# A hybrid decoder layer on one core: norm factors sent through DRAM, gate products in three split passes, and more of the down projection done in seven products of eight

## The chip, the cores and the metric

The kernel runs on one core of a Trainium2 chip. The metric is the device time of one launch in microseconds (us). Before the change it is 2038.34 us, the median of 3 runs (2037.39 to 2038.42). The profiled execution of the same kernel took 2035.2 us, of which 2033.4 us lie between its first and its last instruction (the span).

## The reference

One layer of a decoder is computed for 2048 prompt tokens and 8 single-token samples, 2056 rows of width 1024, all in float32:

```
xn = rmsnorm(x); z = xn @ w_in            # 1024 -> 1792: recurrent branch, gate branch, q, k, v
xc = causal_conv4(xr)
r, i = sigmoid(block_diag(xc, Wa)+ba), sigmoid(block_diag(xc, Wx)+bx)   # 8 blocks of 64 x 64
h_t = a_t h_(t-1) + sqrt(1-a_t^2) (i xc)_t ;  rec = h * gelu(gate)
att = sliding-window attention (self + 128 previous tokens, a sink per head)
mix = [rmsnorm(rec), rmsnorm(att)];  h = x + mix @ w_out
ff = silu(hn @ w_gate) * (hn @ w_up), hn = rmsnorm(h);  y = h + ff @ w_down     # 1024 -> 2816 -> 1024
out = rmsnorm(y)
```

An rmsnorm needs one factor for each token: the inverse root of the mean square of its 1024 (or 512) values.

## The kernel before

**Layout.** Channels lie on the 128 partitions and tokens along the free dimension. A norm factor belongs to a token, so it has to stand in every partition as a row. `rstd_cols` (L1013) sums the squares with TensorE into a column of factors (tokens on partitions); `row_bcast` (L1020) turns such columns into a row on all 128 partitions with one float32 matmul for each 128 tokens (the column spread over 128 weight columns, times the identity) and a ScalarE copy. `half_bcast` (L1042) does the same for the token halves of the feed-forward part.

**Products in split precision.** A float32 operand is split into a high part of type float32r and the rest, also float32r; a product is three matmuls that add up in PSUM: high times high, high times low, low times high. In the trace every matmul of float32r is one record, and a matmul of full float32 is two. The gates of the recurrence (`rec_chunk`, tiles `g`) were not split: one full float32 matmul for each of 40 pieces, 16 of 260 columns and 24 of 512.

**Part one** goes over four runs of tokens (520, 512, 512, 512): input projection (`ip`), convolution, gates, scan, attention (`s`, `pt`, `o`), the two group norms (`rc`, `at`), output projection (`op`), and the sum `h`, which goes to DRAM (`hs`).

**Part two** goes over three groups of tokens (688, 684, 684), each of two halves of 344 or 342 tokens, and in each group over 11 pairs of 128-row pieces of the feed-forward width. Gate and up products (`ps_g`, `ps_u`) take seven products where a two-by-two block product takes eight (the Strassen-Winograd form): 7 x 12 matmuls each, 168 for a pair. The seven sums of `hn` halves (`n`, stored as `mixed` in DRAM by `hn_mix`, read back by `hn_load`) and the seven sums of weight quarters are their operands. The down projection of a pair has two forms:

- `down` (tiles `pd`): the plain eight products, 16 outputs of 6 matmuls, 96 matmuls, and 16 VectorE additions into the running sum `y`. Its weights are split on ScalarE and on GpSimd (`w_d`).
- `down_parts` (tiles `pw`): seven products, 14 rounds of 6 matmuls, 84 matmuls, and 28 VectorE additions into `y`. It needs three more parts of `ff` made of sums (tiles `t`, by additions `c_u<-c_u,c_u`), and sums of weight quarters (`sd`, `rd`), which `down_make` adds up and stores (`sums_d`) and `down_load` reads back.

`wino(gi, p)` (L75) says which pair of which group takes the second form. Before: pairs 1 to 9 of groups 1 and 2; group 0 makes no such sums, group 1 makes and stores them, group 2 reads them. The rounds of pair p stand among the products of pair p+1, from product number `R_AT` on. The lists `E_...` say for each kind of addition whether VectorE (V) or GpSimd (P) does it.

**What sets the order.** All five queues (TensorE, VectorE, ScalarE, GpSimd, and SP, which issues nearly every DMA) run in an order that is written out in the table `ORDER`, one string for each engine; `w_x:17` means 17 instructions recorded under the name `w_x`, and `+2` takes the third one that is still open. Each engine takes its instructions strictly in this order; an instruction that waits holds all that stand behind it.

Of the kernel before, what the change touches and what calls it, by code (L numbers as in the profile page):

```python
# [7 lines left out]
F32 = mybir.dt.float32  # L8
F32R = mybir.dt.float32r
# [44 lines left out]
U_R, R_AT = 0.875, 2  # L54
# [13 lines left out]
E_DSUM = ['P', 'P', 'P', 'P', 'P', 'P', 'P', 'V']  # L68
# [6 lines left out]
def wino(gi, p):  # L75
    return gi > 0 and 0 < p < NPAIR - 1


def plan():
    t, begin, end, prod, down, rounds = T_B0, [], [], {}, {}, {}  # L80
    for gi in range(len(HALVES)):
        begin.append(t)
        for p in range(NPAIR):
            mixed = p and wino(gi, p - 1)
            n = 0
            for i in range(14):
# [12 lines left out]
        end.append(t)  # L99
# [18 lines left out]
vt0_2 ip0_13_0:13 ip0_13_1:6 vt0_3 ip0_13_1:16 ip0_2_0 ip0_13_1 ip0_2_0 ip0_13_1 ip0_2_0:4 s0_0_0:2 ip0_2_0:2 s0_0_0
ip0_2_0 s0_0_0 s0_0_1 ip0_2_0:3 s0_0_1:2 ip0_2_0:3 g0_0_0_0 ip0_2_0:4 s0_0_1 ip0_2_0:4 ip0_2_1:4 s0_1_0 ip0_2_0
ip0_2_1 s0_1_1 s0_1_0:3 ip0_2_1:2 s0_1_1:3 ip0_2_1:2 g0_0_0_260 ip0_2_1:10 s1_0_0 ip0_2_1 s1_0_0:2 ip0_2_1:2 s1_0_0  # L120
ip0_2_1 pt0_0_1 ip0_2_1 pt0_0_1:3 ip0_5_0:2 s1_0_1:2 ip0_5_0:2 s1_0_1:2 ip0_5_0:4 g0_0_1_0 ip0_5_0:10 o0_0_0 ip0_5_0:6
s1_1_0 ip0_5_1:2 s1_1_0:3 ip0_5_1:6 g0_0_1_260 ip0_5_1:3 pt0_1_1:3 ip0_5_1:3 pt0_1_1 o0_0_0 ip0_5_1:2 s1_1_1 ip0_5_1:4
s1_1_1 ip0_5_1 s1_1_1:2 ip0_5_1 ip0_4_0 ip0_5_1:2 ip0_4_0:3 s2_0_0:2 ip0_4_0 s2_0_0 ip0_4_0 s2_0_0 ip0_4_0:4 o0_1_0
ip0_4_0:6 o0_1_0 pt1_0_0 ip0_4_0 pt1_0_0 ip0_4_0:2 pt1_0_0 ip0_4_0:2 pt1_0_0 s2_0_1:4 ip0_4_0 ip0_4_1:2 ip0_4_0
ip0_4_1:6 ip0_4_0 ip0_4_1:16 ip1_8_0:12 ip0_6_0 ip1_8_0:3 ip0_6_0:5 o1_0_0 ip0_6_0:4 pt1_0_1:2 ip0_6_0 ip1_8_0 pt1_0_1
ip0_6_0 o1_0_0 pt1_0_1 g0_3_0_0 ip0_6_0:12 ip0_6_1 ip1_8_0 ip0_6_1:8 ip1_8_0 ip0_6_1:3 s2_1_0 ip0_6_1:3 s2_1_0 ip1_8_0
ip0_6_1 s2_1_0:2 ip0_6_1:4 s2_1_1 ip0_6_1:3 s2_1_1:2 o1_0_1 ip0_6_1 s2_1_1 g0_3_0_260 ip1_8_0:2 pt1_1_0 ip1_8_0
pt1_1_0:2 ip1_8_0 pt1_1_0 ip1_8_0 ip1_9_0:2 o1_0_1 ip1_9_0:9 g0_3_1_0 ip1_9_0:7 ip0_7_0:2 ip1_9_0 ip0_7_0:3 ip1_9_0
ip0_7_0:4 ip1_9_0:3 pt1_1_1:2 o1_1_0 ip1_9_0 ip0_7_0 pt1_1_1:2 o1_1_0 ip0_7_0:4 g0_3_1_260 ip0_7_0:7 s3_0_0 ip0_7_0:3
bc_x1_0 s3_0_0 o1_1_1 s3_0_1 s3_0_0 s3_0_1 s3_0_0 s3_0_1:2 bc_x1_0 pt2_0_0:2 bc_x1_0 pt2_0_0 o1_1_1 ip0_7_1 bc_x1_0  # L130
ip0_7_1:5 pt2_0_0 ip0_7_1:18 o2_0_0 ip1_10_0:4 g0_2_0_0 ip1_10_0:2 o2_0_0 pt2_0_1:3 ip1_10_0:7 pt2_0_1 ip1_10_0:11
ip1_11_0 o2_0_1 ip1_11_0:2 s3_1_0:4 pt2_1_0:2 g0_2_0_260 pt2_1_0 s3_1_1:3 pt2_1_0 ip1_11_0:2 s3_1_1 ip1_11_0 o2_0_1
ip1_11_0:11 pt2_1_1:2 g0_2_1_0 pt2_1_1 ip1_11_0:7 ip1_4_0:4 pt2_1_1 ip1_4_0:2 o2_1_0:2 g0_2_1_260 ip1_4_0:18 ip1_0_0
o2_1_1 ip1_0_0:2 vt1_0 ip1_0_0:5 pt3_0_0:2 ip1_0_0 dS:2 pt3_0_0:2 o2_1_1 ip1_0_0:3 dS ip1_0_0:2 dS:5 ip1_0_0:9 o3_0_0
ip1_12_0 ip1_0_0 dS2 ip1_12_0 dS2 ip1_12_0 pt3_0_1 ip1_12_0 pt3_0_1:2 o3_0_0 pt3_0_1 ip1_12_0:20 ip1_13_0:6 o3_0_1
ip1_13_0:2 o3_0_1 ip1_13_0:2 pt3_1_0:2 ip1_13_0 pt3_1_0 ip1_13_0 pt3_1_0 ip1_13_0:7 dS3 ip1_13_0:3 dS3 ip1_1_0
ip1_13_0:2 ip1_1_0:6 pt3_1_1 ip1_1_0 pt3_1_1:2 o3_1_0 ip1_1_0 pt3_1_1 ip1_1_0 dS4 o3_1_0 dS4 ip1_1_0 dS4 s4_0_0 dS4
ip1_1_0 o3_1_1 s4_0_1:3 s4_0_0:3 s4_0_1 dS4:4 o3_1_1 ip1_1_0:11 ip1_5_0:2 ip1_1_0 dS5 ip1_5_0:2 s4_1_0 dS5 s4_1_1
ip1_5_0 s4_1_1 ip1_5_0 s4_1_0 s4_1_1 ip1_5_0 s4_1_1 ip1_5_0 vt1_1 s4_1_0 ip1_5_0:2 s4_1_0 ip1_5_0:6 pt4_0_0:3
ip1_5_0:2 ip1_2_0 pt4_0_0 s5_0_0 ip1_2_0 s5_0_0:2 s5_0_1:3 s5_0_0 ip1_2_0:2 s5_0_1 vt1_2 ip1_2_0:8 pt4_0_1:4 o4_0_0  # L140
vt1_3 ip1_2_0:5 o4_0_0 ip1_2_0:2 pt4_1_0 st_rc0 ip1_2_0:2 pt4_1_0:3 st_rc0:4 s5_1_0 ip1_2_0:2 s5_1_0:3 ip1_2_0
# [2118 lines left out]
```

## Time and profile before

| what | us |
|---|---|
| median of 3 runs | 2038.34 |
| the profiled execution | 2035.2 |
| its span | 2033.4 |
| TensorE busy in it | 2004.7 |
| VectorE busy | 1472.9 |
| ScalarE busy | 955.0 |
| GpSimd busy | 906.8 |
| part one, until the last output products | 0 to about 663 |
| group 0 of part two, from there | to about 1135 |

Busy time is the union of an engine's instructions. TensorE's matmuls overlap each other (one of 344 columns is recorded with 320 ns, and the next starts 157 ns later), so what a matmul costs is read from the distance of starts or ends, or from the count of matmuls in a stretch, and not from its recorded duration. The granted clock of TensorE is 0.995 over the span.

### The profile page before, as it was taken

Reading aid. Unit: us, or ns where it says so; the run is one execution under the profiler, and the core shown is the slowest. Engines: PE = TensorE matmul, PEld = TensorE weight load, DVE = VectorE, ACT = ScalarE, POOL = GpSimd, SP = SyncE. Lnnn points to the kernel's source line nnn. Section 1 sums busy time; section 2 is a strip of 40 time slices with the busy share of each in tenths; the row PEclk is TensorE's granted clock in tenths of the full one; section 3 lists DMA queues with packets and bytes.
Section 4 is the critical chain, followed back from the end, with each engine's and each line's share of the span. In section 5 each row is a group of like instructions: output and inputs, shape, how many; then the busy total and the mean of one; then the engine's idle time right before and its main releaser. Section 6 shows DMA issues by size and latency. Waiting matters only on the chain.

```text
span 2033.4 us, 34750 instructions
## 1 busy us (share of the span) xinstructions
PE 2004.7 (99%) x12273; PEld 1904.5 (94%) x12273; DVE 1472.9 (72%) x2694; ACT 955.0 (47%) x1960; POOL 906.8 (45%) x799
## 2 busy tenths in 40 slices
PE   9999999999999999999999999999999999999997
PEld 8988887888778999999999999999999999999997
DVE  6888986777886777765555777787767666776675
ACT  5776764654563543443344533343335433433443
POOL 4312451120132796676666645565557422322333
PEclk9999999999999999999999999999999999999999
DMA  9863675667688776764546687776668675555552
GB/s 338 297 215 127 225 273 182 210 197 223 206 288 272 285 245 208 240 212 168 184 172 224 229 282 242 261 240 214 228 209 290 204 236 196 182 197 199 195 173 101
DMA packets 208991, 450.98 MB, mean 222 GB/s; under 512 B 25232, under 2 KB 82720, under 8 KB 208800
## 3 DMA queue, kind: packets, MB, share of 16 engines
q1 hardware_dynamic: 205184, 445.73, 65.2%
q10 hardware_dynamic: 3632, 3.02, 0.5%
q8 instruction: 97, 1.59, 0.3%
q14 instruction: 78, 0.64, 0.1%
HBM read 335.89 MB, written 113.84 MB: 221 GB/s over the span
## 4 chain that ended last, share of the span: by engine, by line
PE 88%; DMA 6%; DVE 4%; issue 1%; ACT 1%; SPq 0%; DVEq 0%; ACTq 0%
PE ps_g L963 20%; PE ps_u L963 20%; PE ip L963 14%; PE pw L963 12%; PE pd L963 11%; PE op L963 5%; PE s L963 1%; DMA m<-mixed 1%; PE g L963 1%; PE pt L968 1%; PE o L963 1%; DMA mixed<-n 1%; DMA y<-hs 1%; DMA xs<-in_xT 0%; DMA hn<-mixed 0%
## 5 line engine op out<-in xcount | busy, mean ns | idle before, releaser
L963 PE MATMUL ps_g<-hn,w_g 128*128 128x342 f32 (+1 forms) x2772 | 546.0, 320 | 1.8 <-DMA w_g<-split_g 1.0
L963 PE MATMUL ps_u<-hn,w_u 128*128 128x342 f32 (+1 forms) x2772 | 529.8, 320 | 4.5 <-ACT c_u L1985 3.5
L963 PEld LDWEIGHTS ps_u<-hn,w_u 128*128 128x128 f32 x2772 | 455.0, 189 | 5.5 <-ACT c_u L1985 3.8
L963 PEld LDWEIGHTS ps_g<-hn,w_g 128*128 128x128 f32 x2772 | 456.6, 189 | 2.5 <-ACT w_d L1778 2.3
L963 PE MATMUL ip<-xn,w_in 128*128 128x512 f32 (+1 forms) x1680 | 367.3, 361 | 3.9 <-ACT w_in L936 2.7
L963 PEld LDWEIGHTS ip<-xn,w_in 128*128 128x128 f32 x1680 | 271.5, 190 | 49.4 <-issue 4.8
L2050 DVE TENSOR_TENSOR y<-y,pw 128x342 f32<-128x342 f32 x504 | 242.7, 506 | 94.8 <-PE pw L963 90.4
L963 PE MATMUL pd<-fh,w_d 128*128 128x344 f32 (+1 forms) x960 | 235.0, 320 | 0.0
L963 PE MATMUL op<-mix,w_out 128*128 128x512 f32 (+1 forms) x960 | 209.8, 362 | 0.3 <-DVE mix L999 0.3
L2021 DVE TENSOR_TENSOR y<-y,pd 128x344 f32<-128x344 f32 (+1 forms) x240 | 119.6, 509 | 103.3 <-PE pd L963 91.1
L963 PEld LDWEIGHTS op<-mix,w_out 128*128 128x128 f32 x960 | 157.6, 190 | 30.0 <-issue 6.1
L963 PE MATMUL pw<-fh,wd 128*128 128x342 f32 x576 | 167.5, 319 | 1.0 <-DVE y L2021 1.0
L963 PEld LDWEIGHTS pd<-fh,w_d 128*128 128x128 f32 x960 | 167.3, 188 | 0.0
L963 PE MATMUL pw<-t,wd 128*128 128x342 f32 x648 | 150.6, 319 | 0.0
L963 PE MATMUL pd<-fl,w_d 128*128 128x344 f32 (+1 forms) x480 | 147.6, 320 | 0.0
L1946 POOL TENSOR_TENSOR c_u<-c_u,c_g 128x342 f32<-128x342 f32 (+1 forms) x60 | 58.8, 980 | 180.2 <-DVE c_u L1964 144.5
L1964 DVE TENSOR_TENSOR c_u<-c_u,ps_u 128x342 f32<-128x342 f32 (+1 forms) x99 | 50.5, 510 | 122.1 <-PE ps_u L963 121.8
L1935 DVE TENSOR_TENSOR fl<-c_u,fh 128x342 fp32r<-128x342 f32 (+1 forms) x132 | 118.5, 909 | 15.3 <-ACT fh L1934 14.2
L1779 POOL TENSOR_TENSOR w_u<-ru,w_u 128x512 fp32r<-128x512 f32 x44 | 58.9, 1340 | 151.8 <-ACT w_u L1778 123.0
L1934 ACT CAST fh<-c_u 128x342 fp32r<-128x342 f32 (+1 forms) x132 | 62.1, 479 | 106.4 <-POOL c_u L1946 41.9
L963 PEld LDWEIGHTS pw<-t,wd 128*128 128x128 f32 x648 | 111.4, 189 | 0.0
L963 PEld LDWEIGHTS pw<-fh,wd 128*128 128x128 f32 x576 | 105.6, 189 | 1.3 <-DVE y L2021 1.3
(299 smaller groups left out, 3499.9 us busy)
## 6 DMA issues: line engine op xcount, KB each, us to landing
w_g<-split_g SPq DMA_DIRECT2D x88, 512.0 KB, 4.4
w_u<-split_u SPq DMA_DIRECT2D x88, 512.0 KB, 5.5
w_in<-split_w SPq DMA_DIRECT2D x84, 512.0 KB, 3.6
rg<-in_wgate SPq DMA_DIRECT2D x110, 256.0 KB, 3.1
ru<-in_wup SPq DMA_DIRECT2D x110, 256.0 KB, 3.3
w_out<-split_w SPq DMA_DIRECT2D x48, 512.0 KB, 4.8
split_g<-w_g SPq DMA_DIRECT2D x44, 512.0 KB, 2.8
split_u<-w_u SPq DMA_DIRECT2D x44, 512.0 KB, 2.9
```

Of the source, the lines that this page charges most:

```text
L963: r = nc.tensor.matmul(*args, **kw)
L968: r = nc.tensor.transpose(*args)
L1779: lo_eng.tensor_tensor(w[:, 1, :], src, w[:, 0, :].bitcast(F32), op=ALU.subtract)
L1934: nc.scalar.copy(hi, v)
L1935: nc.vector.tensor_tensor(lo, v, hi.bitcast(F32), ALU.subtract)
L1946: (nc.vector if p == NPAIR - 1 or src is not v else eng(E_MUL[2 * h + n])).tensor_tensor(v, src, g, op=ALU.mult)
L1964: nc.vector.tensor_tensor(o, a, b, op)
L2021: nc.vector.tensor_tensor(ys[gi, n, m], ys[gi, n, m], ps, ALU.add)
L2050: nc.vector.tensor_tensor(v, v, ps, ALU.add)
```

## The change

**Norm factors.** A new helper, `rows_out`, turns the column of factors into rows with a single TensorE transpose, copies them on ScalarE and writes them to DRAM; `dram_bcast` reads such a row back with a DMA that repeats it on 128 partitions. It takes the place of `row_bcast` for the factors of `x` in token runs 1 to 3, of `rc` in runs 1 and 2, and of the finishing norm of groups 0 and 1. The factors of `h` are written to one row in DRAM (`rows_h`), from which `half_bcast` reads. 56 float32 matmuls go, 13 transposes come, with 13 small writes and 15 reads on SP's queue.

**Gates.** The gate weights are split once (`gwh`, `gwl`), each chunk `xc` is split by ScalarE and GpSimd (`xch`, `xcl`), and a gate piece is three float32r matmuls.

**Down projection.** `wino` now also holds for pair 0 of groups 1 and 2 and for pairs 3 to 9 of group 0. Group 0 makes and stores the weight sums of pairs 3 to 9; group 1 reads these and makes those of pairs 0 to 2; group 2 reads all. In group 0 the sums and splits alternate between VectorE and GpSimd. The rounds of pair 0 start at product number 6 of pair 1 (`R_FIRST`). In all, 864 matmuls `pd` become 756 `pw`.

The scratch that the compiler sets aside for dynamic DMAs is made smaller (2048), and the table `ORDER` is written anew for all engines.

```diff
-U_R, R_AT = 0.875, 2
+U_R, R_AT, R_FIRST = 0.875, 2, 6
...
-E_DSUM = ['P', 'P', 'P', 'P', 'P', 'P', 'P', 'V']
+E_DSUM = [['P', 'V', 'P', 'V', 'P', 'V', 'P', 'V'], ['P', 'P', 'P', 'P', 'P', 'P', 'P', 'V']]
+E_T0 = ['P', 'V', 'P', 'V']
+E_DLO0 = ['P', 'V', 'P', 'V', 'P', 'V', 'P']
...
 def wino(gi, p):
-    return gi > 0 and 0 < p < NPAIR - 1
+    return p < NPAIR - 1 and (gi > 0 or p >= 3)
...
-                if mixed and i >= R_AT:
+                if mixed and i >= (R_AT if p > 1 else R_FIRST):
...
+        rowp = E(tc.tile_pool(name="rowp", bufs=2))
...
+        rows_h = dp.tile([1, NTOK], F32, name="rows_h")
+
+        def rows_out(row, cols, w, nt, name):
+            ps = m_tile(f"tr_{name}")
+            tr(f"tr_{name}", ps[:nt, :w], cols, ident[:w, :w])
+            v = rowp.tile([8, P], F32, tag="row", name=f"row_{name}")[:nt, :w]
+            nc.scalar.copy(v, ps[:nt, :w])
+            nc.sync.dma_start(row.rearrange("o (j p) -> (o j) p", p=w), v)
+
+        def dram_bcast(cols, w, nt, name):
+            row = dp.tile([1, w * nt], F32, name=f"rows_{name}")
+            rows_out(row, cols, w, nt, name)
+            out = bcp.tile([P, TM], F32, tag="bc", name=f"rb_{name}")
+            nc.sync.dma_start(out[:, :w * nt], row.to_broadcast([P, w * nt]))
+            return out
+
+        def h_rows(s):
+            c0, T, _, w, nt = SUBS[s]
+            rows_out(rows_h[:, c0:c0 + T], rs2[:w, s, :nt], w, nt, f"h{s}")
...
         def half_bcast(gi, n, name):
             o, nn = HALVES[gi][n]
             out = hbp.tile([P, TP], F32, tag="hb", name=f"hb_{name}")
-            ps = m_tile(f"hb_{name}")
...
-                        mm(f"hb_{name}", ps[:, x - o:y - o], rs2[:w, s, j:j + 1].to_broadcast([w, P]),
-                                         ident[:w, d0:d0 + y - x], start=True, stop=True)
-            nc.scalar.copy(out[:, :nn], ps[:, :nn])
+            nc.sync.dma_start(out[:, :nn], rows_h[:, o:o + nn].to_broadcast([P, nn]))
             return out
...
-                state[s]["bc"] = row_bcast(cols[:w, :nt], w, nt, f"x{s}")
+                state[s]["bc"] = (dram_bcast if s else row_bcast)(cols[:w, :nt], w, nt, f"x{s}")
...
+                xh = ap1.tile([P, TM], F32R, tag="xch", name=f"xch{s}_{c}")
+                xl = ap1.tile([P, TM], F32R, tag="xcl", name=f"xcl{s}_{c}")
+                nc.scalar.copy(xh[:, :T], xc[:, :T])
+                nc.gpsimd.tensor_tensor(xl[:, :T], xc[:, :T], xh[:, :T].bitcast(F32), op=ALU.subtract)
...
-                            mm(f"g{s}_{c}_{gi}_{n0}", ps[:, :nn], gw[:, (gi * 4 + c) * P:(gi * 4 + c + 1) * P], xc[:, n0:n0 + nn],
-                                             start=True, stop=True)
+                            for i, (w, x) in enumerate(((gwh, xh), (gwl, xh), (gwh, xl))):
+                                mm(f"g{s}_{c}_{gi}_{n0}", ps[:, :nn], w[:, wcols], x[:, n0:n0 + nn], start=i == 0, stop=i == 2)
...
-                bc = row_bcast(cols[:w, :nt], w, nt, name, 0)
+                bc = dram_bcast(cols[:w, :nt], w, nt, name)
...
-                    ch.add(f"wd{gi}.{p}", (down_load if gi == 2 else down_make)(gi, p) if wino(gi, p) else down_weights(gi, p, T_DOWN[gi, p]))
+                    ch.add(f"wd{gi}.{p}", (down_load if gi == 2 or gi and wino(gi - 1, p) else down_make)(gi, p) if wino(gi, p) else down_weights(gi, p, T_DOWN[gi, p]))
```

VectorE at the start of pair 6 of group 0, where the down projection of pair 5 is added in (`c_g0_6` is the gate output of pair 6, `y0` the running sum, `pd0_5`/`pw0_5` the down product in PSUM, `w_u0_6` a split weight). Before:

```order
L1964 TENSOR_TENSOR c_g0_6_00_7212<-c_g0_6_10_7214,ps_g0_6_2_10360 128x344
L2021 TENSOR_TENSOR y0_0_8112<-y0_0_8112,pd0_5_0_0_10468 128x344
L2021 TENSOR_TENSOR y0_0_8112<-y0_0_8112,pd0_5_0_1_10476 128x344
L1964 TENSOR_TENSOR c_g0_6_11_7215<-c_g0_6_11_7215,ps_g0_6_1_10336 128x344
L1779 TENSOR_TENSOR w_u0_6_1_10518<-ru0_6_00_10426,w_u0_6_1_10518 128x512
L2021 TENSOR_TENSOR y0_0_8112<-y0_0_8112,pd0_5_1_0_10484 128x344
L2021 TENSOR_TENSOR y0_1_8121<-y0_1_8121,pd0_5_1_1_10492 128x344
L1779 TENSOR_TENSOR w_u0_6_2_10537<-ru0_6_01_10428,w_u0_6_2_10537 128x512
```

and now:

```order
L2090 TENSOR_TENSOR c_g0_6_00_7376<-c_g0_6_10_7378,ps_g0_6_2_10609 128x344
L1974 TENSOR_TENSOR wd0_5_3_10695<-rd0_5_3_10652,wd0_5_3_10695 128x2x256
L2176 TENSOR_TENSOR y0_3_8312<-y0_3_8312,pw0_5_5_0_10671 128x344
L2176 TENSOR_TENSOR y0_0_8267<-y0_0_8267,pw0_5_1_1_10666 128x344
L2061 TENSOR_TENSOR t0_0_7342<-c_u0_5_11_7375,t0_0_7342 128x344
L2006 TENSOR_TENSOR sd5_5_10769<-rd0_5_3_10652,rd0_5_8_10698 128x256
L2090 TENSOR_TENSOR c_g0_6_11_7379<-c_g0_6_11_7379,ps_g0_6_1_10585 128x344
L2176 TENSOR_TENSOR y0_3_8312<-y0_3_8312,pw0_5_5_1_10676 128x344
L2086 TENSOR_TENSOR c_u0_5_10_7374<-c_u0_5_10_7374,c_u0_5_11_7375 128x344
L1905 TENSOR_TENSOR w_u0_6_2_10790<-ru0_6_01_10626,w_u0_6_2_10790 128x512
L2006 TENSOR_TENSOR sd5_4_10723<-sd5_4_10723,rd0_5_3_10652 128x256
L2061 TENSOR_TENSOR t0_1_7343<-c_u0_5_01_7373,t0_0_7342 128x344
```

Between the first two gate additions stood two instructions, and now five do: weight splits (`wd`), weight sums (`sd`), parts (`t`) and sums of parts (`c_u<-c_u,c_u`) now lie among the additions into `y`. The steps of `hn_mix` for group 1 (the `n` sums), of which 16 stood beside pairs 4 and 5 before, all stand ahead of pair 4 now.

SP's queue where part one ends (`m0_2` are operands of group 0's second product, read from `mixed`; `rows_h` is the row of factors, `hb_1_1` its copy on 128 partitions for group 1). Before:

```order
L1137 DMA m0_2_0_6281<-mixed_113 128x344
L1668 DMA xres3_6_6829<-in_xT 128x512 x2
L1137 DMA m0_2_1_6333<-mixed_113 128x344
L1137 DMA m0_2_2_6371<-mixed_113 128x344
L947 DMA w_out3_5_0_0_6485<-split_w_117 128x1024
L1137 DMA m0_2_3_6376<-mixed_113 128x344
```

and now:

```order
L1253 DMA m0_2_0_6438<-mixed_116 128x344
L1151 DMA rows_h_123<-row_h2_6644 4x128
L1253 DMA m0_2_1_6490<-mixed_116 128x344
L1253 DMA m0_2_2_6528<-mixed_116 128x344
L1173 DMA hb_1_1_8109<-rows_h_123 128x342
L1253 DMA m0_2_3_6533<-mixed_116 128x344
```

The write of the factors and their read now stand between the loads of group 0's operands: SP holds `m0_2_1` until ScalarE has copied the row, and `m0_2_3` until the written row has landed.

More of the change, by code (lines that the diff above doesn't have):

```diff
@@ L1151, in hybrid_step @@
             ap3 = A(tc.tile_pool(name="ap3", bufs=2))
-            gw = ap1.tile([P, 1024], F32, name="gw")
+            gwh = ap1.tile([P, 1024], F32R, name="gwh")
+            gwl = ap1.tile([P, 1024], F32R, name="gwl")
             hist = ap1.tile([P, CR, 3], F32, name="hist")
@@ L1184, in prologue @@
                 nc.sync.dma_start(scv, sconv)
-                nc.sync.dma_start(gw, gatew)
+                raw = bigp.tile([P, 2 * TM], F32, tag="big", name="graw")[:, :1024]
+                nc.sync.dma_start(raw, gatew)
+                nc.scalar.copy(gwh, raw)
+                nc.gpsimd.tensor_tensor(gwl, raw, gwh.bitcast(F32), op=ALU.subtract)
                 nc.sync.dma_start(sh, sh0)
@@ L1409, in group_norm @@
                 rstd_cols(acc[:, :T], w, nt, 1, cols[:w, :nt], f"{name}{s}")
[L1410 removed]
+                bc = (dram_bcast if name == "rc" and s in (1, 2) else row_bcast)(cols[:w, :nt], w, nt, f"{name}{s}")
                 if late:
@@ L1879, in combine @@
                     S[r] = pre[n // 2][:, n % 2]
-                    eng(E_DSUM[(5, 6, 3, 7).index(r) + 4 * half]).tensor_tensor(S[r], a, b, op=op)
+                    eng(E_DSUM[gi][(5, 6, 3, 7).index(r) + 4 * half]).tensor_tensor(S[r], a, b, op=op)
                 for j in range(7):
```

1394 lines of the change are left out of this document (746 added, 648 removed).

## The prediction

> **What bounds the kernel now.** First the page's busy times, its chain, and the view of who waited, for TensorE (PE):
>
> ```profile
> PE 2004.7 (99%) x12273; PEld 1904.5 (94%) x12273; DVE 1472.9 (72%) x2694; ACT 955.0 (47%) x1960; POOL 906.8 (45%) x799
> PE 88%; DMA 6%; DVE 4%; issue 1%; ACT 1%; SPq 0%; DVEq 0%; ACTq 0%
> PE pt L968 <- DVE ptl L1537: 4.4, 4, 2.1
> PE ps_u L963 <- ACT c_u L1985: 3.5, 1, 3.5
> PE ip L963 <- ACT w_in L936: 2.7, 3, 1.6
> ```
>
> TensorE is busy 99%, and its largest waits are a few us in all. Then the stretches, which say where that is true (columns: length; busy us and instructions of PE, PEld, DVE, ACT, POOL; granted clock, DMA share, GB/s):
>
> ```profile
> 200.00:300.00 100.00, 99.42 (x662) 88.49 (x661) 93.97 (x162) 74.29 (x143) 47.85 (x43) 1.00 0.74 251
> 300.00:560.00 260.00, 259.75 (x1251) 209.60 (x1251) 198.87 (x416) 142.43 (x296) 39.98 (x53) 1.00 0.63 203
> 560.00:680.00 120.00, 111.83 (x547) 92.68 (x545) 90.84 (x163) 59.41 (x120) 45.47 (x35) 0.97 0.87 294
> 886.00:1101.00 215.00, 215.00 (x1368) 215.00 (x1367) 121.00 (x189) 84.24 (x162) 133.28 (x101) 1.00 0.51 180
> 1101.00:1200.00 99.00, 96.37 (x627) 95.56 (x626) 69.57 (x106) 44.99 (x100) 58.34 (x52) 1.00 0.80 269
> 1350.00:1550.00 200.00, 200.00 (x1275) 200.00 (x1274) 142.68 (x255) 77.03 (x155) 112.37 (x104) 1.00 0.66 220
> 1650.00:2000.00 350.00, 350.00 (x2229) 350.00 (x2229) 242.64 (x461) 133.72 (x267) 104.52 (x89) 1.00 0.56 187
> ```
>
> In the feed-forward part the matmul comes every 215/1368 = 0.157 us, in group 0 (886 to 1101) as in groups 1 and 2 (200/1275, 350/2229), and TensorE has no idle time. It waits in two places: where part one hands over to part two (560 to 680, 8 us lost, DMA share 0.87), and a little between groups (2.6 us in 1101 to 1200). Between 200 and 300 VectorE (DVE) is busy 94% and TensorE still loses only 0.6 us. So what leaves TensorE leaves the time, as long as no other engine is asked for more than the shortened stretch holds. That condition is the question of this change.
>
> **What TensorE is spared.** Down projection: 864 matmuls become 756; 108 x 0.157 = **17.0 us**, of it 7 x 12 x 0.157 = 13.2 in group 0 and 3.8 in the two first pairs. A pair falls from 264 matmuls (41.4 us) to 252 (39.6 us). For the rest, TensorE's timeline (start, length, matmuls):
>
> ```profile
> 187.74 0.86 PE L963 MATMUL ip<-xn,w_in 128*128 128x512 f32 x3
> 188.43 0.60 PE L968 MATMUL pt<-cs,sc 128*128 128x128 f32 x4
> ...
> 200.81 0.85 PE L963 MATMUL ip<-xn,w_in 128*128 128x512 f32 x3
> 201.51 1.02 PE L963 MATMUL g<-xc,gw 128*128 128x512 f32 x2
> 201.96 1.27 PE L963 MATMUL ip<-xn,w_in 128*128 128x512 f32 x3
> ...
> 302.83 0.39 PE L963 MATMUL o<-ptl,vt 128*128 128x512 f32 x1
> ...
> 1166.56 0.62 PE L963 MATMUL ps_g<-hn,w_g 128*128 128x342 f32 x3
> 1167.02 1.02 PE L963 MATMUL bc_f<-cs,cols_f 86*128 86x86 f32 x8
> 1167.83 0.56 PE L963 MATMUL ps_g<-hn,w_g 128*128 128x342 f32 x2
> ```
>
> A 512-column float32r matmul lasts 0.39 alone, and three end after 0.85, so each adds (0.85 - 0.39)/2 = 0.23. From the end of the third `ip` (201.66) to the end of the later three (203.23) are 1.57 us; less 3 x 0.23 the gate cost 0.88 (two records). Three split passes cost 0.69 to 0.70: 0.17 to 0.19 saved, 24 times, and by columns half of that for the 16 pieces of 260: at 0.165 (I stay at the low side, since the view rounds to 10 ns) 4.0 + 1.3 = **5.3 us**. Broadcasts: from 1167.18 to 1168.39 less 2 x 0.157 leaves 0.90 for four, 0.224 each. 56 go: 12 of x, 8 of rc, 15 of the first two groups' h in part one (7.8 us), 7 of h and 14 of f later (4.7 us); the short ones may be a little cheaper. A transpose costs (189.03 - 188.60)/4 = 0.108; 13 come, 1.4 us. That leaves **11.1 us**, 7.0 of them before 680. In all 17.0 + 5.3 + 11.1 = 33.4 us less for TensorE: 12.3 in part one, 21.1 after it.
>
> **What the others pay.** The mean durations of the added VectorE and GpSimd (POOL) operations, and one of the same kind in three stretches. First 886 to 1101, then 1350 to 1550, then 1650 to 2000:
>
> ```profile
> L2021 DVE TENSOR_TENSOR y<-y,pd 128x344 f32<-128x344 f32 x86 | 43.4, 511 | 47.6 <-PE pd L963 46.5
> L1935 DVE TENSOR_TENSOR fl<-c_u,fh 128x344 fp32r<-128x344 f32 x20 | 20.0, 1006 | 2.3 <-ACT fh L1934 2.1
> ...
> L1935 DVE TENSOR_TENSOR fl<-c_u,fh 128x342 fp32r<-128x342 f32 x20 | 15.9, 808 | 3.2 <-ACT fh L1934 3.2
> L1935 DVE TENSOR_TENSOR t<-c_u,t 128x342 fp32r<-128x342 f32 x15 | 15.2, 1027 | 0.7 <-ACT t L1934 0.7
> L1848 DVE TENSOR_TENSOR wd<-rd,wd 128x512 fp32r<-128x512 f32 x10 | 8.9, 886 | 0.0
> L1946 DVE TENSOR_TENSOR c_u<-c_u,c_g 128x342 f32<-128x342 f32 x5 | 3.2, 649 | 0.1
> L1880 DVE TENSOR_TENSOR sd<-rd,rd 128x256 f32<-128x256 f32 x5 | 3.1, 619 | 0.7 <-DMA rd<-in_wdown 0.7
> L1960 POOL TENSOR_TENSOR c_u<-c_u,c_u 128x342 f32<-128x342 f32 x5 | 5.7, 1131 | 0.7 <-DMA w_g<-split_g 0.5
> L1880 POOL TENSOR_TENSOR sd<-rd,sd 128x256 f32<-128x256 f32 x9 | 7.1, 792 | 1.0 <-DMA rd<-in_wdown 0.5
> ...
> L1935 DVE TENSOR_TENSOR fl<-c_u,fh 128x342 fp32r<-128x342 f32 x35 | 21.2, 609 | 2.2 <-ACT fh L1934 2.2
> ```
>
> *Group 0, pairs 3 to 9.* VectorE needs 121.0/215 x 41.4 = 23.3 us for a pair now. 16 additions into `y` and 7 others read PSUM: 23 x 0.511 = 11.7; the other 11.6 read two tiles of SBUF. To come: 12 additions into `y` (6.1), 3 parts `t` (3.1), 3 weight splits (2.7), 4 weight sums (2.5), 2 sums of parts (1.3): 15.7, together **39.0 us in a pair that TensorE does in 39.6**. And it will not stay at these durations. GpSimd was busy 133.28/215 = 62%; it gets 4 weight sums (3.2) and 2 sums of parts (2.2) more, its splits stay four, so 25.7 + 5.4 = 31.1 of 39.6, 79%. The same subtraction `fl` took 609 ns where GpSimd was busy 30% (104.52/350), 808 at 56%, 1006 at 62%; the additions that read PSUM stay at 511. Carried on along those points, 17 points more would make `fl` about 1.22 us, a fifth longer; all 21.2 us of the two-tile kind (11.6 + 9.6) a fifth longer, beside 17.8 (11.7 + 6.1) from PSUM, is 43.2 us for a pair. Nothing longer at all is 39.0, and TensorE then sets 39.6. The weight splits grew less than `fl` with GpSimd's share, and a pair that gets longer lowers that share again; I take somewhat over a third of the way, **40.6 us**: 7 x (40.6 - 39.6) = 7 us of the 13.2 are lost. What is late then is an addition into `y`: it holds a PSUM bank, and the next round in that bank waits.
>
> The Trainium skill, GPSIMD Engine Reference, Specifications, says that GpSimd shares its SBUF interfaces with VectorE and contends with VectorE instructions that have two SBUF inputs. The three rows of `fl` and the unmoved row of `y` agree with that; by durations without it the sum would be 7 us better, and with it at its fullest it is the second rival below.
>
> *Part one.* GpSimd gets 16 low parts of `xc` and one of the gate weights, ScalarE as many copies; between 200 and 300 VectorE is at 94%, so a few longer instructions there show. The loss at the handover (560 to 680) hangs on DMAs and can keep what arrives early. Between none lost and all 12.3 lost I take 3, since 300 to 560 has 23% of VectorE free.
>
> *Between the groups.* The rounds of pair 0 put 12 more additions and the parts into the pair in which the last group's output is scaled; VectorE was at 70% there (69.57/99). At most the 3.8 us saved go; I take 2.
>
> *The factors' way over DRAM.* These are the nearest DMAs:
>
> ```profile
> w_in<-split_w SPq DMA_DIRECT2D x84, 512.0 KB, 3.6
> xt<-in_xR SPq DMA_DIRECT2D x24, 256.0 KB, 5.0
> out_sconv_o<-xr ACTq DMA_DIRECT2D x4, 4.0 KB, 4.7
> out_sh_o<-q ACTq DMA_DIRECT2D x4, 4.0 KB, 3.0
> ```
>
> A write of 3.0 to 4.7 and a read of about 5 make 8 to 10 us, where a broadcast and a copy took 1 to 2. SP waits for the write before it issues the read, and the weight loads queue behind: five tiles of 12 matmuls x 0.23 give four tiles ahead, 11 us, less 3.6 to land, 7.4 us of cover. A single wait of 3 to 5 us fits into that. I take 0; with cover gone, 8 us for each place that is on the chain.
>
> The sum: 33.4 - 7 - 3 - 2 = 21.4 us. The profiled execution took 2035.2 us; 2035.2 - 21.4 = 2013.8. The median of the runs lies 3.1 above it, so the forecast is **2017 us**.
>
> **Rivals.** *VectorE keeps up* in group 0, and TensorE sets the pace throughout: 7 us more come, 2010. For: 94% with TensorE full between 200 and 300. Against: 39.0 of 39.6 leaves nothing for waits in an engine that works in order.
>
> *VectorE takes over, and the kernel is slower.* Mechanism: with GpSimd at 79%, its work and VectorE's two-tile instructions stretch each other in pairs 3 to 9. At a quarter longer a pair is 17.8 + 21.2 x 1.25 = 44.3 us, longer than the 41.4 of before: 7 x 4.7 = 32.9 lost instead of 7, and 33.4 - 32.9 - 3 - 2 = -4.5, or 2043. It decides from a pair of 43.7 us (break-even: (33.4 - 5)/7 = 4.1 over 39.6). For: the slope of `fl`. Against: GpSimd's share falls when the pair grows.
>
> *The factors come late at the handover.* There `rows_h` and `hb_1_1` stand between the loads of group 0's operands, in the stretch with DMA share 0.87 and 8 us lost already. Late by one trip of 8 us, and half as much more at a group's end: 12 us, 2029. For: nothing there is covered. Against: the loads around it were waiting for DMAs anyway.
>
> **How the numbers follow.** Forecast 2017: 0.40. VectorE keeps up, 2010: 0.28. Late factors, 2029: 0.15. VectorE takes over, 2043: 0.17. A measurement of this kernel tells 0.2% (4 us) from no change: faster is below 2034.3, slower above 2042.4. The first three cases are faster; of the last about half lies above 2042.4 and half within. Faster 0.83, same 0.08, slower 0.09. The range goes from 2003 (all 33.4 saved, and 2 us of the waits at the handover, since every queue's order is new) to 2039, where pairs of 43.7 us, the break-even, would put it; about 0.07 lies below and 0.12 above.
>
> **What the changed profile would show.** Group 0's pairs 4 to 10: the distance between the same products of two pairs is 39.6 (keeps up), 40.6 (forecast) or above 43 (takes over); VectorE's share there 95% or more, `fl` above 1.0 us, and TensorE waiting for `y` or `c_u` of VectorE, which it hardly does now. Part one: the last `op` about 9 us earlier than at 663. Gates: 0.70 for three passes of 512. Handover: idle TensorE in the same place no more than 8 us, or waits for `m<-mixed` and `hb` if the factors are late. The forecast is wrong if VectorE is far from full in group 0, or if TensorE idles where SP holds weight loads.

## The result, and the profile after

The changed kernel takes 2016.23 us (median of 4 runs, 2014.07 to 2018.92) where the kernel before took 2038.12 beside it: a ratio of 0.9894, with a 95% interval of 0.9877 to 0.9911. The forecast was 2017. The total came out as predicted; the parts did not, as the stretches show.

The page of the changed kernel, first busy times, then shares of the chain that ended last:

```profile
PE 1981.0 (98%) x12106; PEld 1882.1 (94%) x12106; DVE 1562.8 (78%) x2894; ACT 979.2 (49%) x2029; POOL 960.3 (48%) x822
PE 91%; DVE 5%; DMA 2%; ACT 1%; issue 1%; POOL 0%; SPq 0%; DVEq 0%; ACTq 0%; POOLq 0%
```

TensorE is still the bound, with 23.7 us less of busy time than before. VectorE got 90 us more.

Now both executions, cut at the same products: end of part one (last `op`), pairs 0 to 2 of group 0, pairs 3 to 10 of group 0, pairs 0 to 2 of group 1, the rest of group 1, pairs 0 to 2 of group 2. Of the two that are left out, pairs 3 to 9 of group 2 take 277.2 and 277.5 us, and the end 75.8 and 77.5. Before:

```profile
0.00:662.80 662.80, 652.08 (x3658) 554.55 (x3659) 525.67 (x1097) 402.21 (x846) 180.64 (x199) 0.99 0.71 235
662.80:773.30 110.50, 106.85 (x669) 105.98 (x668) 79.57 (x109) 51.45 (x101) 87.77 (x62) 0.98 0.72 254
773.30:1105.70 332.40, 332.40 (x2113) 332.40 (x2113) 210.38 (x313) 135.40 (x262) 214.27 (x159) 1.00 0.57 198
1105.70:1236.30 130.60, 127.97 (x828) 127.16 (x827) 96.83 (x154) 54.99 (x120) 78.47 (x71) 1.00 0.80 269
1236.30:1554.30 318.00, 317.62 (x2021) 317.32 (x2020) 235.89 (x412) 122.95 (x246) 181.94 (x166) 1.00 0.70 229
1554.30:1680.40 126.10, 125.06 (x804) 124.75 (x803) 84.92 (x154) 54.04 (x118) 55.84 (x51) 1.00 0.72 242
```

After:

```profile
0.00:657.80 657.80, 645.70 (x3640) 552.81 (x3641) 524.31 (x1097) 406.28 (x861) 203.57 (x216) 0.99 0.72 239
657.80:762.50 104.70, 104.70 (x666) 103.88 (x665) 86.95 (x116) 50.95 (x103) 88.74 (x62) 1.00 0.83 288
762.50:1082.90 320.40, 319.50 (x2021) 317.37 (x2021) 283.53 (x469) 150.79 (x302) 267.68 (x200) 1.00 0.67 231
1082.90:1213.80 130.90, 126.85 (x798) 125.11 (x798) 103.93 (x175) 58.02 (x128) 91.12 (x83) 0.99 0.86 291
1213.80:1530.40 316.60, 316.60 (x2018) 316.60 (x2017) 227.07 (x412) 122.76 (x247) 140.01 (x117) 1.00 0.67 215
1530.40:1657.30 126.90, 123.61 (x781) 122.85 (x781) 92.11 (x170) 55.41 (x122) 59.60 (x53) 0.99 0.75 248
```

The first column of lengths gives the balance:

| stretch | predicted | measured |
|---|---|---|
| part one | -9.3 (12.3 less 3) | -5.0 |
| pairs 0 to 2 of group 0, with the handover | 0 | -5.8 |
| pairs 3 to 10 of group 0 | -6.2 (13.2 less 7) | -12.0 |
| from there to the end | -5.9 (7.9 less 2) | +1.7 (929.4 where it was 927.7) |
| sum | -21.4 | -21.1 |

Group 0 gave nearly everything that leaves TensorE there, and the handover gave something that the forecast had not counted. Part one gave about half of its forecast in this execution, which took 2014.07 us. In four other traces whose part one is the same code (the changed kernel once more, and three experiments that alter only later stretches) the last `op` comes 1.1 to 3.4 us earlier than before the change, not 5.0, so part one's usual gain is nearer 2; the handover and group 0 come out alike in the second trace of the changed kernel (104.4 and 319.5 us). From group 1 on nothing was gained though TensorE has 7.9 us less to do. The waits of TensorE in the changed kernel say where to look:

```profile
PE pw L1071 <- DVE y L2176: 3.9, 2, 3.2
PE ps_u L1071 <- ACT c_u L2111: 3.2, 1, 3.2
PE g L1071 <- ACT ra L1479: 2.7, 1, 2.7
...
PE bc_at L1071 <- ACT rb_at L1141: 1.8, 1, 1.8
```

The first two stand at the ends of groups 0 and 1, the last two in part one, between 200 and 260 us.

### The profile page after: what moved, and what is told of

It reads as the page before. It is cut to its first block, busy times and chain, and to the rows that moved or that the text cites. A ratio compares the mean times of both kernels' runs of the same rounds, so it can differ in the third digit from the quotient of the medians.

```text
span 2012.3 us, 34843 instructions
## 1 busy us (share of the span) xinstructions
PE 1981.0 (98%) x12106; PEld 1882.1 (94%) x12106; DVE 1562.8 (78%) x2894; ACT 979.2 (49%) x2029; POOL 960.3 (48%) x822
## 4 chain that ended last, share of the span: by engine, by line
PE 91%; DVE 5%; DMA 2%; ACT 1%; issue 1%; POOL 0%; SPq 0%; DVEq 0%; ACTq 0%; POOLq 0%
PE ps_u L1071 21%; PE ps_g L1071 21%; PE pw L1071 18%; PE ip L1071 13%; PE op L1071 8%; PE pd L1071 4%; PE o L1071 1%; PE s L1071 1%; PE pt L1076 1%; PE g L1071 1%; DMA rb_f<-rows_f 0%; DVE y L2196 0%; DMA rb_x<-rows_x 0%; DVE xn L1107 0%; DVE y L2245 0%
## 5 line engine op out<-in xcount | busy, mean ns | idle before, releaser
L1071 PE MATMUL ps_u<-hn,w_u 128*128 128x342 f32 (+1 forms) x2772 | 563.1, 321 | 3.3 <-ACT c_u L2111 3.2
L2176 DVE TENSOR_TENSOR y<-y,pw 128x342 f32<-128x342 f32 (+1 forms) x756 | 358.5, 505 | 115.4 <-PE pw L1071 109.3
L1071 PE MATMUL pw<-fh,wd 128*128 128x342 f32 (+1 forms) x864 | 253.9, 320 | 0.1
L1071 PE MATMUL pw<-t,wd 128*128 128x342 f32 (+1 forms) x972 | 243.3, 320 | 4.6 <-DVE y L2176 3.9
L1071 PEld LDWEIGHTS pw<-t,wd 128*128 128x128 f32 x972 | 169.8, 188 | 6.1 <-DVE y L2176 5.1
L1974 POOL TENSOR_TENSOR wd<-rd,wd 128x512 fp32r<-128x512 f32 x85 | 121.0, 1423 | 101.9 <-ACT wd L1973 100.8
L1071 PEld LDWEIGHTS pw<-fh,wd 128*128 128x128 f32 x864 | 158.8, 189 | 0.9 <-DVE y L2176 0.3
L1973 ACT CAST wd<-rd 128x512 fp32r<-128x512 f32 x159 | 98.4, 620 | 120.4 <-PE ps_u L1071 44.2
L1071 PE MATMUL pw<-fl,wd 128*128 128x342 f32 (+1 forms) x432 | 132.7, 320 | 0.0
L1904 ACT CAST w_g<-rg 128x512 fp32r<-128x512 f32 x99 | 60.9, 621 | 70.9 <-issue 26.0
```

The lines of the kernel that those rows point to most:

```text
L1071: r = nc.tensor.matmul(*args, **kw)
L1904: nc.scalar.copy(w[:, 0, :], src)
L1973: nc.scalar.copy(w[:, :, 0], v)
L1974: eng((E_DLO0, E_DLO1, E_DLO2)[gi][j]).tensor_tensor(w[:, :, 1], v, w[:, :, 0].bitcast(F32), op=ALU.subtract)
L2176: nc.vector.tensor_tensor(v, v, ps, ALU.add)
```

## Experiments

All are the changed kernel with one or two things altered; the places of all other instructions in the five queues stay as they are. The changed kernel was timed once more beside the first three:

> The changed kernel unaltered, as the measure for the three others beside it. Its four runs so far lie between 2014.07 and 2018.92 us (median 2016.2). Every theory expects 2014 to 2019 again; the kernel before, beside it, 2037 to 2039.

2016.98 us (2014.96 to 2021.82, 5 runs), ratio 0.9909 [0.9893, 0.9926]. Differences below are against this median; the kernel before stood at 2036.8, 2036.5 and 2035.5 us beside the three batches of runs.

### The factors at the group ends

A stretch of the changed kernel's timeline at the end of group 1 (start, length, engine; in brackets how long the engine stood idle and for whom):

```profile
1597.98 0.24 ACT L1150 COPY row_f<-tr_f 3x114 f32<-3x114 f32 x1 [1.35 <-PE tr_f L1076]
1598.25 0.25 SPq L1151 DMA_DIRECT2D rows_f<-row_f  x1
...
1600.49 0.63 SPq L1157 DMA_DIRECT2D rb_f<-rows_f  x1
...
1605.40 1.92 DVE L2196 SCALAR_TENSOR_TENSOR y<-y,vec,rb_f 128x342 f32<-128x342 f32 x2 [6.38 <-DMA rb_f<-rows_f]
...
1607.24 0.50 DVE L2176 TENSOR_TENSOR y<-y,pw 128x342 f32<-128x342 f32 x1
...
1607.80 0.74 PE L1071 MATMUL pw<-t,wd 128*128 128x342 f32 x3 [3.17 <-DVE y L2176]
```

The row of factors is ready at 1598.22 and back on 128 partitions at about 1605.4: a trip of 7.2 us. VectorE stands at the scaling of `y` for 6.38 us of it. Behind that instruction in VectorE's queue stands an addition of `pw` into `y`, and TensorE needs its PSUM bank. So TensorE waits 3.17 us there for the place of one instruction in VectorE's queue, and not for a lack of time on any engine. The experiment puts the broadcast back on TensorE for these factors alone:

```diff
-                bc = dram_bcast(cols[:w, :nt], w, nt, name)
+                bc = row_bcast(cols[:w, :nt], w, nt, name, 0)
```

> The changed kernel with one part undone: the factors of the finishing norm of groups 0 and 1 come again from TensorE broadcasts (14 matmuls and 4 copies for 4 transposes and 4 round trips through DRAM). Theory: VectorE, in order, waits 13.6 us in four waits for the rows that come back from DRAM, and TensorE loses 7.4 us (3.4 and 0.9 at the end of group 0, 3.3 at the end of group 1) behind it. Undone, about 5 of these 7.4 go (some 2 us were lost there before the change too), 14 x 0.224 - 4 x 0.108 = 2.7 come: 2 to 3 us less than the changed kernel, with no wait of VectorE for the factors over 2 us. Rival: the loss at the group ends comes from the 12 more additions of pair 0, which fill VectorE there; then the stalls stay and the 2.7 come on top: 2 to 3 us more.

2013.39 us (2012.94 to 2014.76), ratio 0.9889 [0.9875, 0.9902]: 3.6 less, where the theory said 2 to 3, though TensorE has 2.7 us more to do. The interval overlaps that of the changed kernel, so the total alone is weak evidence; the stretches are stronger. The two group ends, the changed kernel of the same batch first, then with the factors back:

```profile
1128.00:1216.50 88.50, 82.68 (x523) 80.29 (x523) 68.88 (x125) 30.77 (x65) 51.46 (x48) 1.00 0.86 290
1576.80:1660.30 83.50, 80.20 (x504) 79.45 (x504) 60.71 (x120) 29.38 (x61) 25.17 (x22) 0.98 0.75 243
```

```profile
1129.60:1216.10 86.50, 83.73 (x539) 82.12 (x538) 72.32 (x125) 31.18 (x65) 52.06 (x48) 1.00 0.87 291
1577.50:1658.90 81.40, 80.58 (x515) 79.18 (x514) 60.45 (x120) 29.86 (x61) 25.43 (x22) 1.00 0.74 245
```

TensorE's idle time falls from 5.8 and 3.3 us to 2.8 and 0.8, and no wait for the factors is left. The two stretches together take 171.1 and 172.0 us in the two traces of the changed kernel, and 167.9 here. The additions of pair 0, which the rival blamed, are still there.

### The gates

Two runs take TensorE's three passes back to one full float32 matmul. One also cuts the split of each chunk to 8 columns (shown); the other leaves the split whole, read by nobody.

```diff
-                nc.scalar.copy(xh[:, :T], xc[:, :T])
-                nc.gpsimd.tensor_tensor(xl[:, :T], xc[:, :T], xh[:, :T].bitcast(F32), op=ALU.subtract)
+                nc.scalar.copy(xh[:, :8], xc[:, :8])
+                nc.gpsimd.tensor_tensor(xl[:, :8], xc[:, :8], xh[:, :8].bitcast(F32), op=ALU.subtract)
...
-                            for i, (w, x) in enumerate(((gwh, xh), (gwl, xh), (gwh, xl))):
-                                mm(f"g{s}_{c}_{gi}_{n0}", ps[:, :nn], w[:, wcols], x[:, n0:n0 + nn], start=i == 0, stop=i == 2)
+                            mm(f"g{s}_{c}_{gi}_{n0}", ps[:, :nn], gwh.bitcast(F32)[:, wcols], xc[:, n0:n0 + nn], start=True, stop=True)
```

> The changed kernel with the gates again as one full float32 matmul for each piece (against the high part of the gate weights alone, whose low part is left out of the result), and with the split of each chunk, on ScalarE and GpSimd, cut to 8 of its columns. TensorE pays 5.3 us more; ScalarE is spared 16 copies of 0.6 us and GpSimd 16 subtractions of 1.3 us. Theory A, the splits crowd the engines: part one lost 6.5 us of new TensorE stalls between 80 and 260 us because these copies and subtractions stand in front of other work; without them the stalls go and the time comes out between 1 us below and 1 us above the changed kernel. Theory B, the stalls come with the new order and the other parts: they stay, and the time is 4 to 6 us above the changed kernel.

> As the run with the gates in full float32, but the split of each chunk stays whole on ScalarE and GpSimd and nobody reads it (the low part of the gate weights is again left out of the result). This prices TensorE's share alone: 24 x 0.165 + 16 x 0.08 = 5.3 us above the changed kernel by the count of matmuls, where TensorE sets the pace. By theory A of the other run it lies 5 to 6 us above that run, by theory B within 1.5 us of it. If part one's stalls have slack that swallows TensorE's work, it lies less than 3 us above the changed kernel.

Without the split 2014.12 us (2013.56 to 2014.95), ratio 0.9891 [0.9878, 0.9905], 2.9 less than the changed kernel and below what theory A allowed; with the split left in place 2017.22 (2016.12 to 2018.20), 0.2 more, as the sentence on slack in the expectation had it. So the cheaper gates bring nothing that can be measured, and the split that feeds them costs about 3 us. The interval of the first run overlaps that of the changed kernel, but the traces bear it out: the last addition into `h` of token run 0 ends between 288.6 and 290.8 us in the eight traces with the whole split (the run that only takes the passes back is one of them, at 289.1), at 285.4 and 284.9 in the two without it, and at 286.9 before the change. That addition (with the one before it; start, length) in the changed kernel of the same batch, then in the run without the split:

```profile
289.09 0.76 DVE L1763 TENSOR_TENSOR xres<-xres,op 128x260 f32<-128x260 f32 x2 [0.29 <-PE op L1071]
284.59 0.76 DVE L1744 TENSOR_TENSOR xres<-xres,op 128x260 f32<-128x260 f32 x2
```

The stretch from 200 to 260 us shows one part of how, with VectorE's normalisation `xn` in it; the changed kernel of the same batch, then the one without the split:

```profile
200.00:260.00 60.00, 55.53 (x355) 50.24 (x354) 54.53 (x83) 43.28 (x79) 24.81 (x23) 0.94 0.65 220
L1107 DVE SCALAR_TENSOR_TENSOR xn<-xs,vec,xn 128x512 fp32r<-128x512 f32 x6 | 6.4, 1098 | 0.0
PE g L1071 <- ACT ra L1479: 2.7, 1, 2.7
```

```profile
200.00:260.00 60.00, 57.39 (x384) 50.92 (x383) 56.13 (x88) 44.69 (x83) 25.50 (x25) 1.00 0.68 233
L1089 DVE SCALAR_TENSOR_TENSOR xn<-xs,vec,xn 128x512 fp32r<-128x512 f32 x6 | 5.4, 922 | 0.0
PE g L1053 <- ACT ra L1460: 1.3, 1, 1.3
```

With GpSimd's subtraction gone the same `xn` takes 0.92 instead of 1.10 us, and the wait for `ra` is halved; TensorE's idle time falls from 4.5 to 2.6 us. It is not gone: before the change the same 60 us had 0.2. What is left of it comes with something else in the new order of part one, and that was not taken apart. Nor is `xn` the cause by itself: in the same 60 us before the change it took 1.04 us, nearly as long as with the split.

### The factors of x and rc

```diff
-                state[s]["bc"] = (dram_bcast if s else row_bcast)(cols[:w, :nt], w, nt, f"x{s}")
+                state[s]["bc"] = row_bcast(cols[:w, :nt], w, nt, f"x{s}")
...
-                bc = (dram_bcast if name == "rc" and s in (1, 2) else row_bcast)(cols[:w, :nt], w, nt, f"{name}{s}")
+                bc = row_bcast(cols[:w, :nt], w, nt, f"{name}{s}")
```

> The changed kernel with the factors of x (token runs 1 to 3) and of rc (runs 1 and 2) again from TensorE broadcasts: 20 matmuls for 5 transposes, 20 x 0.224 - 5 x 0.108 = 3.9 us of TensorE more, and 5 round trips through DRAM less. If TensorE sets the pace of part one: 4 us above the changed kernel. If part one has slack that swallows TensorE's work, as the run with TensorE's gates alone said (0.2 us for 5.3 us of work): less than 1 us above. If the waits of VectorE for the rows (2.2 us for x) reach TensorE: 1 to 2 us below.

2019.27 us (2016.30 to 2023.53, 6 runs), 2.3 more, ratio 0.9916 [0.9901, 0.9931]: the interval overlaps that of the changed kernel, and 2.3 lies between the "less than 1" of slack and the 4 of "TensorE sets the pace", so the run settles neither. It speaks against a loss by these trips.

### How much room VectorE has in group 0

Five pairs of group 0 (6 to 10), before and after; the window, and the additions into `y`:

```profile
898.10:1105.70 207.60, 207.60 (x1321) 207.60 (x1320) 115.52 (x180) 84.60 (x164) 129.59 (x98) 1.00 0.51 180
L2021 DVE TENSOR_TENSOR y<-y,pd 128x344 f32<-128x344 f32 x80 | 40.3, 511 | 45.3 <-PE pd L963 44.3
```

```profile
883.70:1082.90 199.20, 199.17 (x1263) 198.49 (x1264) 176.24 (x300) 97.02 (x196) 173.64 (x131) 1.00 0.65 227
L2176 DVE TENSOR_TENSOR y<-y,pw 128x344 f32<-128x344 f32 x140 | 65.3, 502 | 9.0 <-PE pw L1071 8.5
L2061 DVE TENSOR_TENSOR fl<-c_u,fh 128x344 fp32r<-128x344 f32 x20 | 18.7, 937 | 1.5 <-ACT fh L2060 1.3
DVE c_u L2090 <- PE ps_u L1071: 8.6, 6, 3.1
```

A pair takes 199.2/5 = 39.8 us where it took 41.5, and TensorE does not stand still. VectorE is busy 176.24/5 = 35.2 us of it, not 39.0. The durations in the records do add up to 39.2 for a pair (60 instructions); but neighbours overlap in the records, as four instructions in a row show:

```profile
1064.39 0.50 DVE L2176 TENSOR_TENSOR y<-y,pw 128x344 f32<-128x344 f32 x1
1064.82 0.50 DVE L2090 TENSOR_TENSOR c_g<-c_g,ps_g 128x344 f32<-128x344 f32 x1
1065.24 0.50 DVE L2176 TENSOR_TENSOR y<-y,pw 128x344 f32<-128x344 f32 x1
1065.66 1.22 DVE L1905 TENSOR_TENSOR w_u<-ru,w_u 128x512 fp32r<-128x512 f32 x1
```

Each lasts 0.50 and the next starts 0.42 later. That leaves 4.6 us of a pair free. Whether that is room was the question of the next two runs, which move GpSimd's weight sums, and then its splits too, to VectorE:

```diff
-E_DSUM = [['P', 'V', 'P', 'V', 'P', 'V', 'P', 'V'], ['P', 'P', 'P', 'P', 'P', 'P', 'P', 'V']]
+E_DSUM = [['V', 'V', 'V', 'V', 'V', 'V', 'V', 'V'], ['P', 'P', 'P', 'P', 'P', 'P', 'P', 'V']]
...
-E_DLO0 = ['P', 'V', 'P', 'V', 'P', 'V', 'P']
+E_DLO0 = ['V', 'V', 'V', 'V', 'V', 'V', 'V']
```

> The changed kernel with the four weight sums of a pair of group 0 that GpSimd does moved to VectorE (28 instructions, at the same places). VectorE is busy 35.2 us of a pair of 39.8 in the changed kernel, by the union of its records; the durations add up to 39.2, since records of neighbours overlap. Theory U, the union counts: 35.2 + 4 x 0.7 = 38.0, still below 39.8, and the time stays within 1.5 us of the changed kernel. Theory S, the sum of durations counts, as in the prediction: 39.2 + 2.8 = 42.0, VectorE sets 42 us for a pair, and the time is 7 x 2.2 = 15 us more. By both, GpSimd falls from 34.7 to about 30.5 us for a pair, and if its share stretches VectorE's two-tile instructions, the subtraction fl falls from 0.94 to about 0.85 us.

> As the run with the sums on VectorE, and the four splits of GpSimd too (56 instructions moved). Theory U: 38.0 + 4 x 0.9 = 41.6 us, less what the emptier GpSimd (about 25 of 39.8) gives back, some 1.5: 40.1, so VectorE is at its edge: 0 to 6 us more than the changed kernel. Theory S: 45.6 us less 1.5, 30 us more. If VectorE's place in the order matters more than its sum, TensorE waits for additions into y or for c_u in these pairs well before VectorE is full, and more than 6 us come by theory U's numbers.

2028.28 us (ratio 0.9962 [0.9950, 0.9974]), 11.3 more, and 2052.70 (1.0086 [1.0069, 1.0103]), 35.7 more and slower than before the change. The same five pairs, with the sums, then with the splits too:

```profile
890.90:1094.90 204.00, 202.38 (x1262) 198.14 (x1263) 187.06 (x317) 96.79 (x196) 157.05 (x112) 1.00 0.63 219
L2048 DVE TENSOR_TENSOR fl<-c_u,fh 128x344 fp32r<-128x344 f32 x20 | 18.7, 937 | 1.5 <-ACT fh L2047 1.3
DVE c_u L2077 <- PE ps_u L1058: 8.2, 5, 2.9
```

```profile
899.50:1124.20 224.70, 210.61 (x1263) 203.40 (x1264) 207.23 (x337) 96.71 (x196) 128.19 (x92) 0.97 0.57 200
L2049 DVE TENSOR_TENSOR fl<-c_u,fh 128x344 fp32r<-128x344 f32 x20 | 20.6, 1033 | 1.5 <-ACT fh L2048 1.3
DVE c_u L2078 <- PE ps_u L1059: 7.6, 5, 2.9
```

VectorE has 37.4 of 40.8 us for a pair and then 41.4 of 44.9: in both, about 3.5 us of a pair stay idle, and the waits for `ps_u` hardly shrink. These are waits in order, at places where the product that VectorE is to add up isn't there yet. So the room in the changed kernel was not 4.6 us: 2.2 more of work made each of these five pairs 1.0 longer (40.8 for 39.8), and 6.2 more made it 5.1 longer, which leaves about 1 us, and theory U is refuted. (With the sums, 4.8 of the 11.3 us are lost in these five pairs and most of the rest in the pairs before them.) Theory S was near in the totals (15 and 30 foretold) by a sum of the wrong kind.

The two windows refute something else. GpSimd's share falls from 87% (173.64/199.2) to 77% and 57%, and `fl` takes 937, 937 and 1033 ns. The share does not set its duration. Taken one by one in the changed kernel, an `fl` lasts 0.52 us where no GpSimd instruction runs at the time, and a straight line through duration against overlapped time has a slope of 0.7 for the 35 `fl` and `t` of five pairs. (The line alone does not tell cause from effect, since a longer instruction is also overlapped for longer.) What counts is which instructions meet, and the written order makes the same ones meet: a GpSimd instruction runs beside an `fl` for 0.82, 0.87 and 0.86 us on average in the three kernels. Whether GpSimd then still costs time in all was tried by replacing its part of the gate and up weight splits by ScalarE copies, on top of the run with the sums:

```diff
-                lo_eng.tensor_tensor(w[:, 1, :], src, w[:, 0, :].bitcast(F32), op=ALU.subtract)
+                if lo_eng is nc.gpsimd and key[1] == 0:
+                    nc.scalar.copy(w[:, 1, :], src)
+                else:
+                    lo_eng.tensor_tensor(w[:, 1, :], src, w[:, 0, :].bitcast(F32), op=ALU.subtract)
```

> The run with the sums on VectorE (2028.3 us, 11 above the changed kernel, VectorE 37.4 us of a pair of 40.8, GpSimd 31.4), with GpSimd's part of the gate and up weight splits of group 0 replaced by a plain ScalarE copy of the same size, so that these weights' low parts are wrong and GpSimd falls to about 22 us for a pair. VectorE's instructions and their order are the same. Theory C, work on GpSimd stretches VectorE's instructions with two SBUF tiles, by 0.6 to 0.7 us for each us that lies over them: VectorE falls by 2 to 4 us for a pair and TensorE sets the pace again, 2015 to 2019 us. Theory W, VectorE's own order and its waits for TensorE (3.5 us for a pair) make the pair long: 2026 to 2030 us, as with GpSimd full.

```profile
888.90:1090.30 201.40, 200.87 (x1263) 198.17 (x1263) 172.68 (x318) 111.13 (x226) 112.69 (x83) 1.00 0.64 224
L2050 DVE TENSOR_TENSOR fl<-c_u,fh 128x344 fp32r<-128x344 f32 x20 | 15.6, 785 | 1.5 <-ACT fh L2049 1.3
```

2020.42 us (2019.91 to 2021.86): 7.9 of the 11.3 us come back, a little less than theory C foretold. VectorE needs 34.5 us for a pair instead of 37.4 with the same instructions, so theory C carries most of it. GpSimd's share is 56% here (112.69/201.4), about as with the splits moved, but now it runs beside an `fl` for 0.58 us on average, and `fl` takes 785 ns where it took 1033. The rest may be the copies on ScalarE or VectorE's waits in order; the run does not part them.

### Both losses undone

The last run joins the broadcast of the finishing norm's factors by TensorE with gates in full float32 (whole weights, the split cut to 8 columns).

> Two parts of the change undone together: the factors of the finishing norm from TensorE broadcasts, and the gates as one full float32 matmul against the whole gate weights, with the split of each chunk cut to 8 columns that nobody reads. The result is whole. Alone the two were 3.6 and 2.9 us below the changed kernel beside them. If they act in different stages (group ends; part one): 6 to 7 us below the changed kernel, about 2010. If both only remove the same late start, or one of the two differences was scatter: 3 to 4 us below, 2013.

2009.69 us (2008.60 to 2010.60, 4 runs), ratio to the kernel before 0.9872 [0.9857, 0.9888]: 7.3 less than the changed kernel beside the first batch, and faster than both kernels. Its interval lies wholly below that of the changed kernel (0.9893 to 0.9926), so the two losses together are clear of the noise. The two effects add up (3.6 + 2.9 = 6.5), so they sit in different places; the traces say so too, with 167.8 us for the two group ends and the last `op` 6.0 us earlier than before the change.

## Why the prediction was right, and where it was wrong

**TensorE as the bound, and its prices: right.** 0.157 us for a matmul held: 252 of them make 39.6, and a pair takes 39.8. Of 13.2 us in group 0, 12.0 came.

**"It will not stay at these durations", 40.6 us for a pair: wrong by 0.8 us in each of seven pairs.** Two steps failed. The first put single durations (15.7 us) on top of a busy time of 23.3, which is a union in which neighbours overlap; the sum of 39.0 is, by chance of this mixture, the sum of durations (39.2), while VectorE is busy 35.2. The second carried `fl` along GpSimd's share to 1.22 us. GpSimd went past the 79% that I had given it, to 87%, and `fl` took 0.94. VectorE's share is 88% (176.24/199.2), where the forecast named 95% or more. The rival "VectorE keeps up" was the true one for group 0, with about 1 us to spare for a pair: its "against", that 39.0 leaves nothing for waits in an engine that works in order, was the right worry, since VectorE's waits for TensorE take what the overlap gives. The Trainium skill, GPSIMD Engine Reference, Specifications, has GpSimd and VectorE contend over SBUF where VectorE reads two tiles there: the additions from PSUM stayed at 0.50 in every run and `fl` lost 0.15 when GpSimd was relieved, so the rule agrees with the runs, but it gives no share to carry along.

**"I take 3" in part one: 7.3 were lost in the profiled execution and 8.9 to 11.2 in the four other traces, and the 5.3 us for the gates was the term that failed.** It was priced at TensorE alone. Without it 7.0 us were to come from the broadcasts, and in the two traces without the split part one does end 4.9 and 6.0 us earlier than before the change. By the two gate runs the three passes bring 0.2 us where the split stands anyway, and the split itself costs 3.1. Whether the passes lose their 5.3 us to waiting for the split operands was not taken apart. The sentence that "a few longer instructions there show" pointed at the right stretch; `xn` is one of them, by little (1.04 us before, 1.10 now).

**"I take 0" for the factors' way over DRAM: wrong at the group ends.** The trip was estimated at 8 to 10 us and took about 7; the cover was counted for the weight loads behind SP's wait and not for VectorE, which waits for the row itself. That is the rival "the factors come late", at the place that it named second, and it cost 3.6 us, not 12. At the handover, which it named first, nothing came late.

**The handover: 5.8 us gained where I had none.** Before, TensorE stood 3.65 us in the pairs 0 to 2 of group 0 (110.50 less 106.85), nearly all of it in the one wait of 3.5 us for ScalarE's `c_u`, and now not at all, at a higher DMA share (0.83 for 0.72). Which edit did that is open: a run with `h`'s factors back on TensorE was not made.

**"At most the 3.8 us saved go; I take 2" between the groups: about right once the factors are out of the way.** With these back on TensorE, pairs 0 to 2 of groups 1 and 2 take 129.7 and 124.9 us where they took 130.6 and 126.1: 2.1 of 3.8 saved. The last stretch, from pair 10 of group 2 on, got 1.7 us longer (77.5 for 75.8); its cause was not looked for.

So the forecast of the total owed its fit to luck, to errors of both signs: in the profiled execution 11.6 us better than thought in group 0 and at the handover, 11.9 worse in part one and behind group 0.

## What to carry to other kernels

Price an edit on every engine that it touches, not on the bound one: gates that save TensorE 5.3 us of work were worth less than nothing with the split of their operands on ScalarE and GpSimd. A round trip through DRAM is covered only if the instruction that reads the row stands late enough in its own queue; ask what is queued behind it. The idle time of an in-order engine is not room: add work to it, and see whether the waits shrink.

## What the runs showed of the hardware

- VectorE's instructions overlap in the records by about 0.08 us when they follow each other (0.50 long, 0.42 apart), so a sum of durations overstates a full engine: 39.2 against 35.2 us for 60 instructions.
- An instruction of VectorE with two tiles in SBUF (`fl`) took 0.50 to 0.52 us alone (on average, by kernel) and up to 1.6 under a GpSimd instruction, about 0.7 us more for each us overlapped (a line through 35 instructions); GpSimd's own product `c_u<-c_u,c_g` went from 0.95 to about 1.28 us for each. Additions that read PSUM stayed at 0.50 in all of it.
- A row of 342 factors written to DRAM and read back on 128 partitions took 7.2 us from the copy to the first use, at the end of group 1.
